# Tying first products behind dense groups, and putting the next stage's groups in front of the states

## The chip, the core and the metric

The kernel runs on one core of a Trainium2 chip. TensorE (PE) multiplies, VectorE (DVE), ScalarE (ACT) and GpSimd (POOL) work on elements, and SyncE's queue (SP) issues the DMAs. The metric is the device time of one execution in microseconds (us); smaller is better.

## The reference

A trunk of two layers works on a sequence of 1040 rows (16 learned meta rows, then 1024 of x) of 1024 float32 numbers. Each layer does

- `h = h + W_out [HGRN2 heads | gated DeltaNet heads | S5 groups](RMSNorm(h) W_in)`
- `h = h + W2 relu(RMSNorm(h) W1)^2`, with a hidden width of 4096

and a last RMSNorm follows. `W_in` has 3336 columns: four blocks of 256 for HGRN2 (query, forget, input, gate), four of 512 for the DeltaNet (q, k, v, gate z), 8 columns for its rates a and b, and 256 for S5. q, k and v go through a causal convolution of four taps and a silu. The DeltaNet solves, for each chunk, a triangular system made of its keys and decays, and then passes a 128x128 state from chunk to chunk. HGRN2 passes a 64x64 state for each head, S5 a diagonal complex one.

## The kernel before, in words

Activations lie with features on partitions and time along the row. The sequence is cut into two blocks of T=520 columns (b=0, 1), and each layer l is run for one block after the other, so that there are four stages, written (l,b). A block has NW=5 windows of W=104 columns.

**Dense groups.** A product with float32 inputs is made of three fp32r products: each operand is split into a rounded part and a rest (`split`), and `columns` (line 490) adds `wh*xh + wh*xl + wl*xh` over eight 128-row pieces into one of two PSUM buffers `pd`: 48 matmuls to a group. Weights come in granules of 128x512 (`granule`), a DMA, a cast on ACT and a subtraction on DVE or POOL for each. Each stage has 26 groups from `W_in`: 2 for S5 (`in_s5`), 12 for the convolutions (`in_conv`), 4 gates z and 2 HGRN2 gates (`in_gate`), 6 for HGRN2 (`in_hgrn`); `in_rows` makes a and b. `out_mlp` adds `W_out` (8 groups) and the MLP.

**What goes by way of DRAM.** The convolved q, k and v (`qkvd`), the gates (`gated`), the rate rows (`rowd`), the DeltaNet's matrices (`MAd`, and `XD` with the solved diagonal blocks), the HGRN2 rows (`hd`), S5's rows (`ud`, `yd`) and the mixers' outputs (`ydr`) are stored to DRAM and loaded again in other layouts.

**The mixers.** `gdn_begin` (line 816) loads the rate rows and transposes them on PE (line 832); it fills `gtok`, `gsc`, `diag` and `MAd`, which exist once. `gdn_decay` makes the matrices of a window and a pair of heads (10 items), `gdn_solve` (line 912) solves 26-wide diagonal blocks on DVE and stores them to `XD`. `gdn_state` (line 951) does the rest for each of the 10 items: it loads, transposes k and v (lines 973 and 974), multiplies the matrix by the solved blocks (line 987), copies a transposed quarter on ACT (line 993), and carries the state of its pair from window to window; its result is stored at line 1054. `hgrn` (line 1179) begins with three products with a constant block matrix (line 1205). `s5_layer` (line 336) makes a layer's S5 matrices, mostly on DVE; `s5` runs beside the state items.

**The order.** The program's calls give priorities, and a planner makes each engine's queue from them: of the instructions whose inputs are ready by its own clock and for whose tile a buffer is free, the first in program order goes next. Each engine then runs its queue in that order, and waits where data come later than planned. Tiles of one tag share a number of buffers: `s` 6, `mt` 11, `qt` 2, `D2` 3, `ys` 3, `xh` and `xl` 8 each. `after` (line 127) can tie one instruction of an engine behind another in the queue, without a wait.

**The stages.** `block` runs (0,0), (0,1) and (1,1): `normed_rows` makes a stage's normed and split operands (16 tiles), `projection` runs its groups and mixers, and `states` its DeltaNet and S5 states. Then `out_mlp(0,0)` follows; `projection(1,0)` is interleaved with `out_mlp(0,1)`; then `states(1,0)`, stage (1,1), and `out_mlp(1,b)` for both blocks. The operands of a stage lie in `xh` and `xl`, but those of (1,0) in the idle tiles of the states (`spare_operands`: `mt`, `qt` and `D2`). A function `early`, traced inside `projection(0,0)`, loads x of block 1 through tiles `s`, turns it on PE (line 1306) and saves it.

## Time and profile before

| | |
|---|---|
| median of 3 runs | 2977.9 us (2974.53 to 2978.24) |
| the profiled execution | 2977.42 us |
| its span, first to last instruction | 2975.6 us |
| PE busy in the span | 2809.2 us (94%) |
| DVE, ACT, POOL busy | 58%, 44%, 27% |
| mean granted clock of PE | 0.97 |

The page gives busy times over the whole span, and then 40 slices with a digit for tenths. PE is busy nearly everywhere, but not in the first slices, around the ninth, and where the DeltaNet's solve of a stage stands. A granted clock of 0.5 is 1.2 GHz, of 1.0 is 2.4 GHz; a value between is a mean over a stretch.

### The profile page before, as it was taken

To read this page: it belongs to the slowest core of one execution; us is meant where nothing else is said; L and a number is where in the kernel's file an instruction comes from. 1 tells how busy PE (TensorE), PEld (TensorE's weight loads), DVE (VectorE), ACT (ScalarE), POOL (GpSimd) and SP (SyncE) were. 2 spreads that over 40 slices of the span, in tenths; PEclk is the share of its full clock that TensorE was granted. 3 is DMA by queue.
4 is the path that set the end of the run, shared out by engine and by line. 5 is a ranking of instruction groups with operands and counts; after the bars stand their busy time and mean duration, and the time that the engine had idled before them with its cause. 6 is when DMAs were issued, how large, how long until landed. Compare 5 with 4: busy or idle time off the path is not lost.

```text
span 2975.6 us, 60318 instructions
## 1 busy us (share of the span) xinstructions
PE 2809.2 (94%) x23513; PEld 2623.8 (88%) x23513; DVE 1715.3 (58%) x3505; ACT 1308.8 (44%) x2690; POOL 816.0 (27%) x793
## 2 busy tenths in 40 slices
PE   7797899979999999998999998999899999999998
PEld 6697798878999999998999988997777788999998
DVE  7788885775532246668765677669645323622224
ACT  5455475534443344443443446554344333533332
POOL 0000532154634420000020320112636444144441
PEclk8898999989999999999999999999899999999999
DMA  5666655744433344444543456564534333533332
GB/s 152 187 150 180 168 147 153 192 88 127 121 88 108 91 139 122 127 125 103 160 125 101 120 161 161 156 195 116 133 112 113 89 105 96 162 93 93 92 91 82
DMA packets 641610, 381.17 MB, mean 128 GB/s; under 512 B 166239, under 2 KB 599237, under 8 KB 641325
## 3 DMA queue, kind: packets, MB, share of 16 engines
q1 hardware_dynamic: 641325, 377.31, 46.0%
q8 instruction: 186, 3.05, 0.4%
q14 instruction: 99, 0.81, 0.1%
HBM read 308.52 MB, written 70.43 MB: 127 GB/s over the span
## 4 chain that ended last, share of the span: by engine, by line
PE 76%; DVE 12%; DMA 6%; issue 2%; ACT 2%; POOL 1%; SPq 1%; DVEq 0%; ACTq 0%; POOLq 0%
PE pd L125 65%; PE mxt L125 7%; DVE mh L113 4%; PE mxh L125 3%; DVE s L116 1%; DVE wl L113 1%; DVE s L113 1%; DMA nt<-rowd 1%; DMA ys<-ydr 1%; DMA XD<-diag 1%; ACT s L110 1%; DMA nh<-rowd 1%; DMA wr<-in_mlp_w_dram 0%; DVE h L113 0%; DVE mt L113 0%
## 5 line engine op out<-in xcount | busy, mean ns | idle before, releaser
L460 ACT CAST wh<-wr 128x512 fp32r<-128x512 f32 x776 | 479.8, 619 | 963.2 <-PE pd L125 883.2
L125 PE MATMUL pd<-xh,wh 128*128 128x260 f32 (+4 forms) x3336 | 751.6, 298 | 26.9 <-ACT wh L460 7.2
L125 PE MATMUL pd<-xl,wh 128*128 128x260 f32 (+4 forms) x3336 | 751.6, 298 | 4.5 <-DVE xl L113 2.6
L125 PE MATMUL pd<-xh,wl 128*128 128x260 f32 (+2 forms) x3288 | 737.4, 297 | 1.8 <-DVE wl L113 1.0
L113 POOL TENSOR_TENSOR wl<-wr,wh 128x512 fp32r<-128x512 f32 x368 | 488.7, 1329 | 730.4 <-ACT wh L460 697.4
L125 PEld LDWEIGHTS pd<-xh,wh 128*128 128x128 f32 (+1 forms) x3336 | 531.4, 190 | 47.3 <-ACT wh L460 11.5
L125 PEld LDWEIGHTS pd<-xl,wh 128*128 128x128 f32 (+1 forms) x3336 | 533.0, 190 | 20.4 <-DVE xl L113 3.4
L125 PEld LDWEIGHTS pd<-xh,wl 128*128 128x128 f32 x3288 | 526.1, 191 | 17.0 <-POOL wl L113 2.2
L125 PE MATMUL pd<-uh,wh 128*128 128x260 f32 (+1 forms) x1928 | 456.8, 305 | 17.3 <-DVE h L113 16.3
L125 PE MATMUL pd<-uh,wl 128*128 128x260 f32 (+1 forms) x1928 | 455.8, 304 | 0.0
L125 PE MATMUL pd<-ul,wh 128*128 128x260 f32 (+1 forms) x1928 | 453.8, 304 | 1.0 <-DVE ul L113 1.0
L113 DVE TENSOR_TENSOR h<-h,pd 128x520 f32<-128x520 f32 (+2 forms) x296 | 200.0, 677 | 327.7 <-PE pd L125 325.5
L113 DVE TENSOR_TENSOR wl<-wr,wh 128x512 fp32r<-128x512 f32 x408 | 285.2, 700 | 105.1 <-ACT wh L460 91.1
L125 PEld LDWEIGHTS pd<-uh,wh 128*128 128x128 f32 x1928 | 310.9, 190 | 33.5 <-DVE h L113 10.4
L125 PEld LDWEIGHTS pd<-uh,wl 128*128 128x128 f32 x1928 | 310.9, 190 | 14.2
L125 PEld LDWEIGHTS pd<-ul,wh 128*128 128x128 f32 x1928 | 310.6, 190 | 14.1 <-DVE ul L113 1.6
L110 ACT ACTIVATE s<-s 128x520 f32<-128x520 f32 (+3 forms) x431 | 272.2, 636 | 111.5 <-DVE s L121 51.8
L116 DVE SCALAR_TENSOR_TENSOR s<-pd,r 128x520 f32<-128x520 f32 (+2 forms) x121 | 83.5, 691 | 249.6 <-PE pd L125 249.0
L113 DVE TENSOR_TENSOR s<-s 128x520 f32<-128x520 f32 (+3 forms) x199 | 137.9, 696 | 51.0 <-ACT s L110 48.3
L113 DVE TENSOR_TENSOR ul<-s,uh 128x520 fp32r<-128x520 f32 (+1 forms) x129 | 94.7, 737 | 115.3 <-ACT uh L460 114.8
L113 POOL TENSOR_TENSOR nt<-nt 128x208 f32<-128x208 f32 x80 | 58.0, 725 | 348.7 <-ACT nt L110 209.6
L403 POOL MEMSET mh<- 128x512 f32 x2 | 1.1, 526 | 499.0 <-DVE RT L113 299.0
(275 smaller groups left out, 3527.0 us busy)
## 6 DMA issues: line engine op xcount, KB each, us to landing
wr<-in_mlp_w_dram SPq DMA_DIRECT2D x512, 256.0 KB
wr<-in_w_in_dram SPq DMA_DIRECT2D x208, 256.0 KB
wr<-in_w_out_dram SPq DMA_DIRECT2D x64, 256.0 KB
qkvd<-s SPq DMA_DIRECT2D x48, 260.0 KB
win<-qkvd SPq DMA_DIRECT2D x40, 312.0 KB
hdr<-h SPq DMA_DIRECT2D x32, 260.0 KB
mh<-qkvd SPq DMA_DIRECT2D x40, 208.0 KB
hd<-s SPq DMA_DIRECT2D x32, 260.0 KB
```

Of the source, the lines that this page charges most:

```text
L110: return self.nc.scalar.activation(out, in_, func, **kw)
L113: return (eng or self.nc.vector).tensor_tensor(out, a, b, op)
L116: return self.nc.vector.scalar_tensor_tensor(out, a, s, b, op0, op1)
L125: return self.nc.tensor.matmul(out, lhsT, rhs, start=start, stop=stop, **kw)
L403: nc.gpsimd.memset(z, 0.0)
L460: self.nc.scalar.copy(hi, src)
```

## The change

1. `columns` keeps its last matmul in `self.dense`, and a new `pin` ties an instruction behind it in PE's queue. Tied are: the transposes of the rate rows in `gdn_begin`; in `gdn_state` the transposes of k and the first product of the first item alone; and the three block products at the start of `hgrn`.
2. In `projection`, `gdn_begin` comes behind the first two convolutions instead of ahead of them; a gate z follows every two of the first eight convolutions; `s5_layer` stands behind the last four; both `in_hgrn` stand ahead of the HGRN2 gates and mixers.
3. The first groups of the next stage are traced in front of the states: `in_s5` of (0,1) before `states(0,0)`, two `W_out` groups of `out_mlp(0,0)` before `states(0,1)`, `in_s5` of (1,1) before `states(1,0)`, two `W_out` groups of `out_mlp(1,0)` before `states(1,1)`. `block` is gone; its parts stand in `run`.
4. Stage (0,0) puts its operands in the spare tiles, and its sum of squares is made on PE: 16 products with the matrix of ones into PSUM, in place of seven additions on DVE and two such products.
5. x of block 1 is loaded through tiles `ys` instead of `s`.

```diff
@@ -128,6 +128,11 @@
         self.tc.add_manual_dep(later.ins, first.ins.name,
                                mybir.DependencyInfo(mybir.DependencyClass.NoSync, mybir.DependencyReason.DATA),
                                reason="accumulation groups of one bank")
+
+    def pin(self, ins):
+
+        self.after(ins, self.dense)
+        return ins
 
     def tl(self, pool, shape, tag, bufs, dt=F32):
         return pool.tile(shape, dt, tag=tag, name=tag, bufs=bufs)
@@ -494,8 +499,8 @@
             wh, wl = wts[k // 4]
             for i, (w, x) in enumerate(((wh, xh), (wh, xl), (wl, xh))):
                 for c, cs in runs.items():
-                    self.mm(ps[:, c, :cs.stop - cs.start], w[:, k % 4, :], x[k][:, cs],
-                            start=(k == 0 and i == 0), stop=(k == kn - 1 and i == 2))
+                    self.dense = self.mm(ps[:, c, :cs.stop - cs.start], w[:, k % 4, :], x[k][:, cs],
+                                         start=(k == 0 and i == 0), stop=(k == kn - 1 and i == 2))
         return ps
 
     def operand(self, tag):
@@ -507,16 +512,28 @@
             for _ in range(bufs):
                 yield self.tl(self.sp, [128, T + HIST], tag, bufs, F32R)
 
-    def normed_rows(self, h, wcol, b, spare=None, acc=None):
+    def normed_rows(self, h, wcol, b, spare=None, acc=None, first=False):
 
         nc = self.nc
         xs = [], []
-        if acc is None:
-            acc = self.s()
+        self.squares, self.r = acc, None
+        if first:
+            self.squares = []
+            for k in range(KD):
+                self.squares.append(self.s())
+                self.act(self.squares[k], h[k], AF.Square)
+                if k == 0:
+                    ps = self.tl(self.pd, [128, 2, 512], "pd", 2)
+                for c in range(2):
+                    self.mm(ps[:, c, :HN], self.K["ones"], self.squares[k][:, self.run_of(c)], start=(k == 0), stop=(k == KD - 1))
+            self.r = self.tl(self.sp, [128, T], "r", 1)
+            self.act(self.half(self.r), ps[:, :, :HN], AF.Ln, scale=1.0 / D, bias=EPS)
+            self.act(self.r, self.r, AF.Exp, scale=-0.5)
+        elif acc is None:
+            self.squares = acc = self.s()
             for k in range(KD):
                 self.square(acc, h[k], k)
-        self.squares, self.r = acc, None
-        r = self.scale("t" if spare else None)
+        r = self.scale("t" if spare and not first else None)
         if b == 0:
             self.hist = self.tl(self.big, [128, KD, HIST], "hist", 1)
         for k in range(KD):
@@ -725,14 +742,6 @@
                     return
             yield
 
-    def block(self, l, b, h, hook=None, first=False, acc=None):
-
-        xs = self.normed_rows(h, 8 * l, b, acc=acc)
-        if first:
-            self.save_h(b, h)
-        trace(self.projection(l, b, xs, hook, first))
-        self.states(l, b)
-
     def projection(self, l, b, xs, hook=None, first=False):
 
 
@@ -746,40 +755,46 @@
         g["rows"] = self.in_rows(l, b, xs)
         yield MIX
         g["qkv"] = self.QKV = self.tl(self.dr, [12, 128, T], "qkvd", 2)
-        self.gdn_begin(l, b, g)
         for p in range(2):
-            for i in (2 * p, 2 * p + 1, 4 + 2 * p, 5 + 2 * p):
+            for n, i in enumerate((2 * p, 2 * p + 1, 4 + 2 * p, 5 + 2 * p)):
                 self.in_conv(l, b, xs, i)
                 yield DENSE
+                if p == 0 and n == 1:
+                    self.gdn_begin(l, b, g)
+                if n % 2:
+                    z = 2 * p + n // 2
+                    self.in_gate(l, xs, C_GZ + 128 * z, g["z"][z])
+                    yield DENSE
             for _ in pipeline([self.gdn_decay(g, w, p) for w in range(NW)], GAP_DECAY):
                 yield MIX
         self.gdn_solve()
         self.gdn_scales()
-        if b == 0:
-            self.s5_layer(l)
         if hook:
             trace(hook)
         for i in range(8, 12):
             self.in_conv(l, b, xs, i)
             yield DENSE
-        for i in range(4):
-            self.in_gate(l, xs, C_GZ + 128 * i, g["z"][i])
-            yield DENSE
+        if b == 0:
+            self.s5_layer(l)
+        hd = []
+        for j in range(2):
+            hd.append(self.in_hgrn(l, xs, j))
+            yield 3 * DENSE
+        self.Y = self.YS[b]
         for j in range(2):
             if j and (l, b) != (1, 0):
                 self.grp = "t"
                 self.loaded = self.s5_load(0, us[0])
                 self.grp = "h"
-            hd = self.in_hgrn(l, xs, j)
-            yield 3 * DENSE
             self.in_gate(l, xs, C_HG + 128 * j, g["z"][4 + j])
             yield DENSE
-            for _ in self.hgrn(l, b, j, hd, g["z"][4 + j]):
+            for _ in self.hgrn(l, b, j, hd[j], g["z"][4 + j]):
                 yield MIX
         self.mixed = g, us
 
     def states(self, l, b):
         g, us = self.mixed
+        self.Y = self.YS[b]
         self.grp = "t"
         trace(pipeline([self.gdn_state(l, g, w, p) for w in range(NW) for p in range(2)], GAP_STATE),
               self.lead(self.s5(l, b, us), AHEAD_S5))
@@ -829,7 +844,7 @@
         for w0, n in ((0, 4), (4, 1)):
             ps = self.mps()
             for i in range(n):
-                nc.tensor.transpose(ps[:W, i * 68:(i + 1) * 68], rows[:68, (w0 + i) * W:(w0 + i + 1) * W], self.ident[:68, :68])
+                self.pin(nc.tensor.transpose(ps[:W, i * 68:(i + 1) * 68], rows[:68, (w0 + i) * W:(w0 + i + 1) * W], self.ident[:68, :68]))
             for i, c in enumerate((0, 36, 64)):
                 nc.scalar.copy(tok[:, w0:w0 + n, i], ps[:W, :n * 68].rearrange("p (a b) -> p a b", a=n)[:, :, c:c + 4])
         sc = self.tl(self.sp, [W, NW, 4, 4], "gsc", 1)
@@ -970,14 +985,18 @@
         ps = self.mps()
         ps4 = ps[:W].rearrange("p (a b c) -> p a b c", a=2, b=2)
         for h in range(2):
-            nc.tensor.transpose(ps4[:, 0, h, :], qkv[:, 2 + h, :], self.ident)
+            first = nc.tensor.transpose(ps4[:, 0, h, :], qkv[:, 2 + h, :], self.ident)
+            if w + pair == 0:
+                self.pin(first)
             nc.tensor.transpose(ps4[:, 1, h, :], qkv[:, 4 + h, :], self.ident)
         kv = self.m()[:W, :512].rearrange("p (a b c) -> p a b c", a=2, b=2)
         self.tt(kv, ps4, sc[:, w, 0:2, hs].unsqueeze(3).to_broadcast([W, 2, 2, 128]), ALU.mult)
         yield
         ps = self.mps()
         for h in range(2):
-            self.mm(p2(ps)[:, h, :], M[:, h, :], XT[:, h, :])
+            first = self.mm(p2(ps)[:, h, :], M[:, h, :], XT[:, h, :])
+            if w + pair == 0:
+                self.pin(first)
         Pm = self.n([W, 2, W])
         self.tt(Pm, p2(ps), K["lev"].unsqueeze(1).to_broadcast([W, 2, W]), ALU.mult)
         yield
@@ -1202,7 +1221,7 @@
         for src, dst, val in ((P[:, :HN], ho[:, :HN], v[:, :HN]), (P[:, HN:], ho[:, HN:], v[:, HN:]), (f, g_, odd(v, 0))):
             ps = self.mps()
             for i, part in enumerate(self.parts(src)):
-                self.mm(ps[:, :HN], K["blk"], part, start=(i == 0), stop=(i == 1))
+                self.pin(self.mm(ps[:, :HN], K["blk"], part, start=(i == 0), stop=(i == 1)))
             self.tt(dst, ps[:, :HN], val, ALU.mult)
             yield
         self.tt(odd(ho, 1), odd(ho, 1), g_, ALU.add, eng=nc.gpsimd)
@@ -1294,7 +1313,7 @@
         for w in range(NW):
             t0 = b * T + w * W - NMETA
             for k0 in (0, 4):
-                xt = self.s()[:W, :512]
+                xt = (self.tl(self.sp, [128, T], "ys", 3) if b else self.s())[:W, :512]
                 cs = slice(128 * k0, 128 * k0 + 512)
                 if t0 < 0:
                     nc.sync.dma_start(xt[0:NMETA, :], self.ins["meta"][:, cs])
@@ -1503,15 +1522,25 @@
         trace(self.load_x(0, h))
         self.ready = {(0, col): self.in_weights(0, col) for col in (C_SU, C_SU + 128)}
         self.setup_norms()
-        self.block(0, 0, h, early(), True)
-        self.block(0, 1, nxt[1])
-        h = self.get_h(0)
+        xs = self.normed_rows(h, 0, 0, self.spare_operands(), first=True)
+        self.save_h(0, h)
+        trace(self.projection(0, 0, xs, early(), True))
+        xs = self.normed_rows(nxt[1], 0, 1)
+        nxt = self.projection(0, 1, xs)
+        next(nxt)
+        self.states(0, 0)
+        trace(nxt)
         ys = []
 
         def before():
             self.low = None
             ys.append(self.y_operands(1, 0))
-        trace(self.out_mlp(0, 0, h, before=before))
+        h = self.get_h(0)
+        nxt = self.out_mlp(0, 0, h, before=before)
+        for _ in range(2):
+            next(nxt)
+        self.states(0, 1)
+        trace(nxt)
         self.low = None
         xs = self.normed_rows(h, 8, 0, self.spare_operands(), self.acc)
         self.save_h(0, h)
@@ -1528,14 +1557,24 @@
         trace(rest)
         acc = self.acc
         self.save_h(1, h)
+        xs = self.normed_rows(h, 8, 1, acc=acc)
+        nxt = self.projection(1, 1, xs)
+        next(nxt)
         self.states(1, 0)
-        self.block(1, 1, h, acc=acc)
+        trace(nxt)
+
         for b in range(NB):
-
             self.take(512 if b == 0 else T)
             h = self.get_h(b)
             self.steps = None
-            trace(self.out_mlp(1, b, h, b == 1))
+            nxt = self.out_mlp(1, b, h, b == 1)
+            if b == 0:
+                for _ in range(2):
+                    next(nxt)
+                self.take(T)
+                self.states(1, 1)
+                self.take(512)
+            trace(nxt)
             self.low = None
             self.finish(b, h, self.steps)
```

## Rows read from the trace of the kernel before

**Rows 1.** The page's span, busy times, and slices of PE, POOL and PE's clock.

```profile
span 2975.6 us, 60318 instructions
...
PE 2809.2 (94%) x23513; PEld 2623.8 (88%) x23513; DVE 1715.3 (58%) x3505; ACT 1308.8 (44%) x2690; POOL 816.0 (27%) x793
...
PE   7797899979999999998999998999899999999998
...
POOL 0000532154634420000020320112636444144441
PEclk8898999989999999999999999999899999999999
```

**Rows 2.** Who PE waited for, whole span: us in total, times, longest.

```profile
PE pd L1306 <- DMA s<-in_x_dram: 15.0, 6, 8.9
PE mxt L125 <- DMA mt<-MAd: 13.1, 2, 8.5
PE mxh L832 <- DMA mh<-rowd: 11.1, 4, 8.0
```

**Rows 3.** Timeline, 20 to 31 us, sum of squares: start, us, engine, line, tiles.

```profile
25.93 0.70 DVE L113 TENSOR_TENSOR s<-s 128x520 f32<-128x520 f32 x1
...
26.69 2.10 PE L125 MATMUL pd<-s,ones 128*128 128x260 f32 x4 [6.20 <-DVE s L113]
...
29.52 0.58 ACT L110 ACTIVATE r<-pd 128x520 f32<-128x520 f32 x1
```

**Rows 4.** Timeline of PE at 1833 us: the same products elsewhere.

```profile
1833.42 1.04 PE L125 MATMUL mxt<-mt,ones 128*128 128x260 f32 x4
```

**Rows 5.** Windows of 10 us: PE, PEld, DVE, ACT, POOL busy, PEclk, DMA.

```profile
110.00:120.00 10.00, 3.07 (x16) 2.61 (x16) 10.00 (x28) 5.64 (x17) 0.00 (x0) 0.58 0.56 153
120.00:130.00 10.00, 5.19 (x24) 3.85 (x24) 4.56 (x15) 3.88 (x13) 0.00 (x0) 0.50 0.81 229
130.00:140.00 10.00, 7.14 (x41) 6.52 (x40) 4.63 (x16) 2.92 (x14) 0.00 (x0) 0.55 0.72 156
```

**Rows 6.** Timeline of SP, 117 to 132 us: loads of x.

```profile
118.96 0.82 SPq L1303 DMA_DIRECT2D s<-in_x_dram  x2
```

**Rows 7.** Windows of 10 us at the end of (0,0)'s groups.

```profile
250.00:260.00 10.00, 1.41 (x5) 0.72 (x5) 9.77 (x18) 6.50 (x16) 0.00 (x0) 0.58 0.10 28
260.00:270.00 10.00, 5.34 (x17) 3.79 (x18) 7.26 (x12) 5.87 (x13) 0.00 (x0) 0.50 0.54 176
```

**Rows 8.** Timeline of SP: last store of `s5_layer`; last store of `states(0,0)`.

```profile
305.14 0.54 SPq L456 DMA_DIRECT2D D<-D  x1
...
553.35 0.37 SPq L1054 DMA_DIRECT2D ydr<-nt  x1
```

**Rows 9.** Window of 10 us at the rate rows of (1,1).

```profile
1820.00:1830.00 10.00, 2.03 (x13) 1.81 (x12) 4.88 (x10) 2.58 (x9) 0.00 (x0) 0.76 0.48 125
```

**Rows 10.** Timeline of PE: first product (line 987) of `states(1,0)`.

```profile
1732.83 0.53 PE L125 MATMUL mxt<-mt 104*104 104x104 f32 x4
```

**Rows 11.** Timeline of ACT: line 993, once an item, in `states(1,0)`.

```profile
1755.20 0.23 ACT L993 COPY nt<-mxt 52x104 f32<-52x104 f32 x1
1782.77 0.24 ACT L993 COPY nt<-mxt 52x104 f32<-52x104 f32 x1
1841.30 0.24 ACT L993 COPY nt<-mxt 52x104 f32<-52x104 f32 x1 [1.30 <-PE mxt L991]
...
1971.39 0.24 ACT L993 COPY nt<-mxt 52x104 f32<-52x104 f32 x1
```

**Rows 12.** Timeline of SP: second `in_s5` of (1,1); last store of `states(1,0)`.

```profile
1791.22 0.35 SPq L161 DMA_DIRECT2D ud<-s  x1
...
1994.42 0.55 SPq L1054 DMA_DIRECT2D ydr<-nt  x1
```

**Rows 13.** Timeline of DVE: five like products of the solves of (0,1) and (1,0).

```profile
630.13 7.61 DVE L113 TENSOR_TENSOR mh<-nh,Tm 80x507 f32<-80x507 f32 x5
...
1386.36 4.43 DVE L113 TENSOR_TENSOR mh<-nh,Tm 80x507 f32<-80x507 f32 x5
```

## The prediction, made before the changed kernel ran

> **What bounds the kernel now.** I read the busy times and slices first. PE works 2809.2 of 2975.6 us [rows 1], so all that can be won without removing products is 166.4 us of idle PE, and the time its products lose at the half clock; in the slices both lie mostly at the start, in the first eighth. Next I read whom PE waited for. Three DMAs stand out, each waited for in the middle of PE's queue by a product that the planner placed too early: x of block 1 (15.0 us), `MAd` (13.1) and the rate rows (11.1) [rows 2]. Then I went through the trace in windows, to see in each hole what else was at its limit, since a hole in which DVE is full does not close when PE's wait goes. Last I looked for the chains that let the next big supply of dense groups begin: stage (0,0) leads by way of `s5_layer`, whose last store is at 305.14, to `states(0,0)`, which store last at 553.35 [rows 8]; `states(1,0)` store last at 1994.42 [rows 12]. Only then can the `W_out` groups of either layer's block 0 have all their operands. A hole closed before such a point is won only if the chain comes sooner too.
>
> **1. Sum of squares on PE.** Before, seven additions of 0.70 us stand on DVE, the last ends at 26.63, the products with ones take 2.10 us at the half clock, and the normalizer starts at 29.52 [rows 3]. After, 16 products run instead of 2: eight times the work. At full clock the same pair takes 1.04 us [rows 4], so all sixteen take between 8.3 and 16.8 us. They can start with the first square, which was there before the additions began at 26.6 − 4.9 = 21.7, say at 21. Result: between 29 and 38 in place of 28.8. Against that, PE works without a break before the first dense group, so that group should no longer begin at the half clock, and DVE loses 4.9 us of work. Bounds −5 to +8; I take **−2**, near the full-clock end.
>
> **2. x of block 1 through `ys`.** From 110 to 140 PE is busy 3.07 + 5.19 + 7.14 = 15.4 us of 30, at a granted clock near 0.54 [rows 5]. The loads go out from 118.96 on [rows 6], when tiles `s` come free from the convolutions, and PE's queue is blocked behind their transposes. The ten loads themselves stay, in SP's one queue; with three buffers of their own they can be issued whenever SP passes them, though a load that waits for its `ys` buffer holds the weight granules behind it. All the idle is 14.6 us, and the products at half clock cost about 7 more: lower end −21. But DVE was busy 10.00 + 4.56 + 4.63 of these 30 us, and in the first ten it was the full engine, so only its 10.8 idle us can be won. Upper end +3, if three buffers in place of six make the loads trickle. I take **−11**.
>
> **3. Spare operands for (0,0).** Operands of (0,1) no longer wait for the last groups of (0,0). Between 250 and 270 PE is busy 6.75 us of 20; DVE 17.03 [rows 7]. PE could win 13.2, DVE leaves 3.0. I take **−3**, bounds −13 and 0. The spare tiles are those of the states, but these start only behind `s5_layer` anyway, and the last readers of the spare operands, the HGRN2 gates, are dense groups without a wait of their own.
>
> **4. Rate rows tied behind two convolutions.** In (1,1) PE is busy 2.03 us of 10 in the window from 1820, mostly because of the longest wait for rate rows, 8.0 us [rows 2, 9]. Two groups in front cover it; what queues behind the transposes (the decays) needs them anyway. About 1.5 us go back through the clock (0.76 there). In (0,1) `gtok` comes free only with the last state, far behind the convolutions, so there the tie does nothing. I take **−9**; bounds −13 (all 11.1 and the clock) and 0.
>
> **5. Ties in `gdn_state` and `hgrn` at the other stages.** The product that waits 8.5 us for `MAd` [rows 2] belongs to (0,1), and the other one, 4.6 us of the 13.1, to (1,1). Their tie is to the second `W_out` group. In (0,1) the operands of that group are there soon after 553.35 [rows 8], while the solve that feeds the waiting product still runs at 630 [rows 13]. The group is out of the queue long before, and a tie behind something done moves nothing. **0**; lower end −13, the case in which the planner saves these groups up.
>
> **6. `states(1,0)` behind `in_s5` of (1,1).** Here the tie acts. The first item's product ran at 1732.83 [rows 10], as filler beside the end of the MLP; now it stands behind a group whose output was stored at 1791.22 [rows 12]: up to 58 us later. These items are a chain: from the third of the ten to the last, (1971.39 − 1841.30)/7 = 18.6 us an item [rows 11]. But from the first to the third it was 1755.20 to 1841.30, 86 us, where two times 18.6 = 37 us would do: the normalization, S5's own end and the rate-row stall lay between. Starting 58 us late and needing up to 49 less, the chain ends 9 to 58 us late; and only pair 0 is tied, so pair 1's items can go ahead, which takes the delay towards nothing. Bounds 0 and +58. Whatever it is comes through in full, since behind 1994.42 the next groups wait for this chain. I take **+7**, near the 9, since the steady 18.6 us hold for eight of the ten items, and a little less for pair 1.
>
> **7. Order inside the stages.** Gates z between convolutions, both `in_hgrn` first, `s5_layer` later: the same instructions and DMAs, in an order in which a light drain (gate) follows two heavy ones on DVE. `s5_layer` moves past convolutions that ran ahead of most of it anyway. **0**, bounds −8 and +12. The upper end is from the solves: five like DVE products took 7.61 us in (0,1), in a slice where POOL is half busy, and 4.43 in (1,0), where POOL is idle [rows 1, 13], 1.7 times as much; if all 17 DVE us of the two windows of [rows 7] came to stand beside POOL, that would be 12 us. The Trainium skill (SBUF — State Buffer, Who interferes with whom) has the rule: a DVE instruction with two SBUF inputs contends with a GpSimd instruction that reads SBUF. By that rule a later `s5_layer`, beside the POOL work of `hgrn(0,0)`, is a loss of those 12 us; the order of calls, `s5_layer` ahead of `hgrn`, speaks against it.
>
> **Sum.** −2 −11 −3 −9 +0 +7 +0 = −18. The profiled execution took 2977.4 us, of which 1.8 lie outside the span; it is 0.5 below the median, so 2977.9 − 18 = **2960**.
>
> **Rivals.** *A: the ties do all they say.* The planner leaves two groups in front of each first product, also in (0,1) and (1,1): the 13.1 us for `MAd` go, and the late start of step 6 costs nothing, 2960 − 13 − 7 = 2940, with the rest of step 2 some 2933. For it: the waits are real and in-queue [rows 2]. Against: step 5. *B: slower.* `states(1,0)` start 58 us late and pair 1 does not go ahead, because the waiting items hold the buffers; little of the 49 us is caught up. Step 6 then costs about 45 instead of 7: 2998. It turns to slower when step 6 exceeds the 25 us of the other steps. For it: the chain's end meets the end of the dense supply. Against: the first items were slow because of their company. *C: nothing arrives.* Steps 1 to 3 win 16 us of PE time early, but `s5_layer` ends no sooner than 305, `states(0,0)` no sooner than 553, and PE waits there instead: 2960 + 16 = 2976. For it: DVE is full at 110 and at 250 [rows 5, 7]. Against: its idle 10.8 us.
>
> **How the numbers follow.** This measurement can tell about 0.2% (6 us) from no change. Forecast 0.46, its own range 2940 to 2975, of which 0.05 lies within 6 us of before; A 0.19; B 0.18; C 0.17, of which 0.03 faster, 0.10 the same, 0.04 slower. Faster 0.41 + 0.19 + 0.03 = 0.63; same 0.05 + 0.10 = 0.15; slower 0.18 + 0.04 = 0.22. The range for all reaches from inside A to inside B, 2924 to 2995.
>
> **What would show it.** Step 1: a normalizer start near 29 and a first dense group at full clock. Step 2: no wait for `in_x` over 2 us, and block 1's transposes spread over the groups. Step 3: the normalization of (0,1) inside the groups of (0,0), and no hole behind their end. Step 4: the wait for rate rows below 3 us in all. Step 5: waits for `MAd` as before in (0,1) and (1,1). Step 6: the first product at line 987 of `states(1,0)` behind that stage's `in_s5`, and the last store not over 10 us later, counted from the end of the MLP. The prediction is wrong if PE idles more than 15 us ahead of `W_out` of either block 0 (B or C), or if the holes near the solves close too (A).

## The result, and the profile after

The changed kernel takes 3004.2 us (median of 6 runs, 3000.8 to 3010.5) against 2979.8 us of the kernel before in the same runs: a ratio of 1.0082, interval [1.0071, 1.0094]. It is slower by 24 us, where 18 us less was forecast and 2995 was the top of the range. The page of the changed kernel begins so (compare [rows 1]):

```profile
span 3004.1 us, 60347 instructions
...
PE 2836.9 (94%) x23541; PEld 2648.2 (88%) x23541; DVE 1708.5 (57%) x3498; ACT 1309.7 (44%) x2690; POOL 805.5 (27%) x793
...
PE   8897999889999999999799999999899999999998
...
PEclk8998999889999999999999999998999999999999
```

PE's busy time grew by 27.7 us with 28 more records, and its idle time is 167.2 us where it was 166.4. Two things are mixed in this. The 28 records are the new products of step 1, which ran in a stretch where PE had idled before (in [rows 3] they are 4 records and 2.10 us):

```profile
18.65 10.27 PE L125 MATMUL pd<-s,ones 128*128 128x260 f32 x32 [0.33 <-DVE h L1328]
32.07 1.24 PE L125 MATMUL pd<-mt,wh 128*128 128x264 f32 x4 [3.16 <-ACT mt L550]
```

In the first 40 us PE is busy for 28.73 us instead of 21.97. Behind them it idles 7.5 us longer than before and is busy 20.9 us longer, with two records fewer. So most of the loss shows as busy time, where it is easily missed: products that run at the half clock are busy for twice as long (2.10 against 1.04 us in [rows 3, 4]). So I cut both executions at the same four events (`states(0,1)` done, out_mlp(0,1) done, `states(1,0)` done, `states(1,1)` done) and at the first output store. Before (columns as in [rows 5]):

```profile
894.00:1756.00 862.00, 838.82 (x7504) 824.66 (x7502) 496.86 (x968) 356.70 (x661) 135.25 (x136) 0.99 0.43 121
1756.00:1994.00 238.00, 224.65 (x1814) 214.61 (x1815) 164.73 (x323) 136.06 (x300) 32.59 (x39) 0.98 0.63 168
1994.00:2386.00 392.00, 373.41 (x2578) 297.35 (x2578) 227.01 (x448) 166.77 (x375) 177.34 (x173) 0.97 0.44 118
2386.00:2548.00 162.00, 161.68 (x769) 132.42 (x768) 58.36 (x91) 61.59 (x104) 67.80 (x54) 1.00 0.39 118
```

After:

```profile
902.00:1761.00 859.00, 829.34 (x7391) 816.89 (x7391) 488.27 (x942) 354.07 (x656) 130.73 (x129) 0.99 0.43 120
1761.00:2026.00 265.00, 253.49 (x1983) 238.51 (x1983) 176.78 (x356) 142.24 (x313) 38.51 (x46) 0.94 0.60 163
2026.00:2401.00 375.00, 353.68 (x2463) 281.02 (x2463) 213.48 (x432) 159.60 (x357) 170.16 (x169) 0.95 0.43 116
2401.00:2576.00 175.00, 174.68 (x830) 142.82 (x829) 62.52 (x99) 66.90 (x114) 72.84 (x58) 1.00 0.38 116
```

Up to the end of out_mlp(0,1) the changed kernel has lost 5 us. From there to the first output store it takes 265 + 375 + 175 = 815 us where 238 + 392 + 162 = 792 did: 23 us more. Two things are in it. The stretch up to the end of out_mlp(0,1) ran 113 products fewer (7504 to 7391) and became only 3 us shorter; they run later instead, at 838.8/7504 = 0.11 us each some 12 us. And the granted clock fell in both stretches up to `states(1,1)`: one minus the clock, times the length, is 238 x 0.02 + 392 x 0.03 = 17 us before and 265 x 0.06 + 375 x 0.05 = 35 us after. That is 18 us at most, as the column is rounded and a part of it lies over idle PE.

The place is seen in windows of 10 us about the end of `states(1,0)`. The changed kernel:

```profile
2000.00:2010.00 10.00, 8.19 (x58) 6.52 (x56) 4.86 (x12) 4.93 (x12) 0.62 (x1) 1.00 0.60 141
2010.00:2020.00 10.00, 8.31 (x32) 6.91 (x33) 3.32 (x10) 3.05 (x9) 1.87 (x3) 0.56 0.31 82
2020.00:2030.00 10.00, 4.59 (x32) 3.94 (x30) 5.20 (x16) 4.23 (x13) 0.62 (x1) 0.84 0.63 163
2030.00:2040.00 10.00, 7.85 (x26) 6.14 (x27) 8.00 (x23) 4.29 (x13) 0.00 (x0) 0.50 0.71 196
```

The kernel before, 10 us earlier in its run:

```profile
1990.00:2000.00 10.00, 10.00 (x88) 9.76 (x87) 9.54 (x28) 6.06 (x18) 0.64 (x1) 1.00 0.68 201
2000.00:2010.00 10.00, 9.45 (x46) 7.34 (x44) 8.97 (x22) 6.19 (x16) 0.00 (x0) 1.00 1.02 310
2010.00:2020.00 10.00, 8.55 (x40) 7.23 (x41) 8.54 (x18) 6.24 (x14) 0.00 (x0) 0.83 0.71 180
```

Before, the chain of `states(1,0)` ends at 1994 while PE still has groups of (1,1), and the `W_out` groups take over. After, the groups of (1,1) and the first few `W_out` products are used up at about 2004, the chain ends at 2026, and in between PE has mostly the small products of the items: it is partly idle, its clock falls to 0.56 and, after 2030, to 0.50, and `W_out` products run at that clock. The timeline of SP and PE in the changed kernel gives the chain (compare [rows 8, 10, 12]): the last store of `s5_layer` and of `states(0,0)`; the last store of `h` by out_mlp(0,1); the first product of `states(1,0)`; the second `in_s5` of (1,1); the last store of `states(1,0)`.

```profile
318.65 0.55 SPq L461 DMA_DIRECT2D D<-D  x1
...
563.45 0.36 SPq L1073 DMA_DIRECT2D ydr<-nt  x1
...
1760.78 0.34 SPq L166 DMA_DIRECT2D hdr<-h  x1
...
1787.15 0.53 PE L125 MATMUL mxt<-mt 104*104 104x104 f32 x4
1787.79 0.46 SPq L166 DMA_DIRECT2D ud<-s  x1
...
2025.77 0.36 SPq L1073 DMA_DIRECT2D ydr<-nt  x1
```

The other holes of the changed kernel, first by whom PE waited for, as in [rows 2]:

```profile
PE mxt L125 <- DMA mt<-MAd: 13.1, 2, 9.0
...
PE pd L125 <- DVE s L113: 9.5, 1, 9.5
...
PE mxh L847 <- DMA mh<-rowd: 5.5, 3, 2.6
...
PE pd L1325 <- DMA s<-in_x_dram: 2.3, 2, 2.0
...
PE pd L1325 <- DMA ys<-in_x_dram: 1.4, 1, 1.4
```

Then by windows, as in [rows 5, 7, 9]:

```profile
110.00:120.00 10.00, 10.00 (x87) 10.00 (x87) 10.00 (x25) 6.62 (x19) 0.00 (x0) 1.00 0.63 161
...
130.00:140.00 10.00, 7.13 (x60) 6.56 (x58) 8.16 (x17) 7.61 (x18) 0.00 (x0) 1.00 0.66 173
140.00:150.00 10.00, 3.96 (x20) 3.37 (x21) 3.19 (x11) 1.84 (x9) 0.00 (x0) 0.54 0.74 210
150.00:160.00 10.00, 7.69 (x48) 6.77 (x48) 8.49 (x30) 4.98 (x22) 0.00 (x0) 0.67 0.68 195
...
240.00:250.00 10.00, 2.64 (x23) 2.43 (x21) 9.80 (x43) 8.05 (x16) 0.00 (x0) 0.83 0.59 145
250.00:260.00 10.00, 3.31 (x8) 2.11 (x8) 9.90 (x27) 5.29 (x13) 0.52 (x1) 0.50 0.48 111
260.00:270.00 10.00, 9.58 (x68) 9.58 (x69) 9.91 (x29) 2.87 (x7) 0.53 (x1) 0.82 0.48 145
...
1820.00:1830.00 10.00, 7.13 (x51) 6.59 (x51) 6.79 (x11) 4.70 (x14) 3.77 (x5) 0.85 0.66 187
```

The window from 240 in the kernel before, which stands ahead of those of [rows 7]:

```profile
240.00:250.00 10.00, 7.51 (x63) 7.30 (x61) 9.88 (x35) 4.42 (x8) 0.00 (x0) 1.00 0.72 174
```

The waits that the change was aimed at did fall: for x from 15.0 to 3.7 us, for rate rows from 11.1 to 5.5. The holes did not go with them. The one from 110 to 140 stands at 130 to 160 now, the one from 250 to 270 at 240 to 260.

### The profile page after: what moved, and what is told of

It reads as the page before. It is cut to its first block, busy times and chain, and to the rows that moved or that the text cites. A ratio compares the mean times of both kernels' runs of the same rounds, so it can differ in the third digit from the quotient of the medians.

```text
span 3004.1 us, 60347 instructions
## 1 busy us (share of the span) xinstructions
PE 2836.9 (94%) x23541; PEld 2648.2 (88%) x23541; DVE 1708.5 (57%) x3498; ACT 1309.7 (44%) x2690; POOL 805.5 (27%) x793
## 4 chain that ended last, share of the span: by engine, by line
PE 77%; DVE 11%; DMA 6%; issue 3%; ACT 2%; SPq 0%; POOL 0%; DVEq 0%; ACTq 0%; POOLq 0%
PE pd L125 65%; PE mxt L125 8%; DVE mh L113 3%; PE mxh L125 3%; DVE s L116 1%; DVE wl L113 1%; DVE s L113 1%; ACT s L110 1%; DMA XD<-diag 1%; DMA nh<-rowd 1%; DVE h L113 0%; DMA mh<-rowd 0%; DVE mt L113 0%; DMA rowd<-s 0%; DMA nt<-rowd 0%
## 5 line engine op out<-in xcount | busy, mean ns | idle before, releaser
L125 PE MATMUL pd<-xh,wh 128*128 128x260 f32 (+3 forms) x2904 | 665.2, 301 | 12.6 <-DVE s L116 4.6
L125 PE MATMUL pd<-xl,wh 128*128 128x260 f32 (+3 forms) x2904 | 662.8, 300 | 6.2 <-DVE xl L113 3.5
L125 PE MATMUL pd<-xh,wl 128*128 128x260 f32 (+2 forms) x2872 | 656.0, 300 | 1.0 <-POOL wl L113 1.0
L125 PEld LDWEIGHTS pd<-xh,wh 128*128 128x128 f32 (+1 forms) x2904 | 466.6, 191 | 31.3 <-ACT xh L550 4.9
L125 PEld LDWEIGHTS pd<-xl,wh 128*128 128x128 f32 (+1 forms) x2904 | 468.3, 191 | 22.1 <-DVE xl L113 4.3
L125 PEld LDWEIGHTS pd<-xh,wl 128*128 128x128 f32 x2872 | 463.5, 192 | 16.6 <-POOL wl L113 2.1
L125 PE MATMUL pd<-mt,wh 128*128 128x264 f32 (+3 forms) x1188 | 206.9, 295 | 24.9 <-DVE h L113 5.6
L125 PEld LDWEIGHTS pd<-mt,wh 128*128 128x128 f32 (+1 forms) x1188 | 173.6, 195 | 28.3 <-issue 9.1
```

What stands on the lines that cost most here:

```text
L125: return self.nc.tensor.matmul(out, lhsT, rhs, start=start, stop=stop, **kw)
```

## The experiments

Each ratio is against runs of the kernel before on the same chip. The edits are cut to the lines that matter: `...` marks a gap, and lines that only serve others (`pin`, `self.dense`, `self.Y`) are left out. Landmarks are from one profiled execution each. M is the last store of `h` by out_mlp(0,1). It fell between 1754.6 and 1769.3, and between 1756.2 and 1763.5 even in kernels whose program text differs only behind it, so times near the end are counted from M. The table collects all kernels, by where `states(1,0)` stand in the program and how soon their first product ran.

| kernel | first product, from M | last store of `states(1,0)`, from M | ratio |
|---|---|---|---|
| before | -23 | 238 | 1 |
| b1, b2 (before + one part) | -23, -23 | 238, 239 | 1.0012, 0.9998 |
| h2 (before, items put ahead) | -26 | 231 | 0.9993 |
| f1, g4: behind `in_s5`, no state tie | -24, -24 | 241, 240 | 1.0012, 1.0008 |
| b3: states first, new inner order | -1 | 239 | 1.0001 |
| e1, e6: states first, all ties | -1, -1 | 241, 242 | 1.0032, 1.0019 |
| o1: states first, all ties, old inner order | 0 | 253 | 1.0061 |
| g3: behind `in_s5`, new inner order, no tie | -1 | 258 | 1.0069 |
| e2, g2: behind `in_s5`, no state tie | -1, -1 | 251, 253 | 1.0051, 1.0075 |
| f2: behind `in_s5` and tied | 24 | 260 | 1.0072 |
| the changed kernel | 26 | 265 | 1.0082 |
| e3, e4, e5, g1 (changed - one part) | 26, 25, 26, 27 | 262, 260, 267, 263 | 1.0094, 1.0079, 1.0088, 1.0095 |
| h1 (changed, items put ahead) | 26 | 268 | 1.0102 |

From the last store of `states(1,0)` to the end of the span it is 971 to 981 us in all twenty kernels, so what a kernel loses here it has lost by that store. From M to the end of the span it is 1210 to 1219 us in the nine kernels whose chain ends by 242, and 1223 to 1243 in the eleven whose chain ends at 251 or later.

**Where `states(1,0)` stand: e1 and f1.** e1 is the changed kernel with the states in front again.

```diff
+        self.states(1, 0)
         xs = self.normed_rows(h, 8, 1, acc=acc)
         nxt = self.projection(1, 1, xs)
-        next(nxt)
-        self.states(1, 0)
         trace(nxt)
```

> The changed kernel with one place undone: states(1,0) are traced ahead of the normalization and of in_s5 of (1,1), as before; all ties stay. Theory 'late chain' (the 28 us are lost because the states of (1,0) begin behind in_s5 of (1,1), so that W_out of layer 1's block 0 gets its operands late): the last store of states(1,0) comes 20 to 32 us sooner, and the time falls from 3004 to 2972 to 2984. Rival 'clock' (the loss is spread: PE at the half clock more often, no one place): the time stays within 8 us of 3004.

Measured: 1.0032 [1.0017, 1.0046]. The timelines of PE and SP give the first product and the last store of `states(1,0)` in e1:

```profile
1754.00 0.53 PE L125 MATMUL mxt<-mt 104*104 104x104 f32 x4
...
1996.11 0.46 SPq L1073 DMA_DIRECT2D ydr<-nt  x1
```

Its windows behind that end:

```profile
2000.00:2010.00 10.00, 8.38 (x63) 7.75 (x62) 8.70 (x22) 6.71 (x18) 0.00 (x0) 1.00 0.85 227
2010.00:2020.00 10.00, 10.00 (x57) 8.36 (x57) 9.97 (x25) 6.92 (x17) 0.00 (x0) 1.00 0.92 273
```

The hole at the end of the chain is gone, and with it more than half of the loss (0.82% to 0.32%). f1 is the opposite: the kernel before with that one move.

```diff
-        self.states(1, 0)
-        self.block(1, 1, h, acc=acc)
+        xs = self.normed_rows(h, 8, 1, acc=acc)
+        nxt = self.projection(1, 1, xs)
+        next(nxt)
+        self.states(1, 0)
+        trace(nxt)
+        self.states(1, 1)
```

> The kernel before, with one edit: normalization and in_s5 of (1,1) are traced in front of states(1,0); no tie anywhere. Theory 'two parts' (the place of states(1,0) behind in_s5 costs by itself, and the tie adds to it): the last store of states(1,0) comes 10 to 18 us later than 1994, at 2004 to 2012, and the ratio is 1.003 to 1.006. Rival 'the tie is needed' (the planner takes the first items as filler anyway, as soon as a buffer is free): last store at 1994 to 1999, ratio 0.999 to 1.002.

Measured: 1.0012 [0.9997, 1.0027], no difference that can be measured. The first item still ran as filler beside the MLP, at 1739.47. So the move is needed for most of the loss, but does not make it by itself.

**Move and tie: f2.** f1 and the state ties of the changed kernel, nothing else.

```diff
-            nc.tensor.transpose(ps4[:, 0, h, :], qkv[:, 2 + h, :], self.ident)
+            first = nc.tensor.transpose(ps4[:, 0, h, :], qkv[:, 2 + h, :], self.ident)
+            if w + pair == 0:
+                self.pin(first)
...
-            self.mm(p2(ps)[:, h, :], M[:, h, :], XT[:, h, :])
+            first = self.mm(p2(ps)[:, h, :], M[:, h, :], XT[:, h, :])
+            if w + pair == 0:
+                self.pin(first)
```

> As f1, and the first item of gdn_state is tied behind the last dense group as in the changed kernel (in the other stages that group is long done). Theory 'two parts': 12 to 16 us more than f1, last store of states(1,0) at 2016 to 2026, ratio 1.007 to 1.011: this alone is then the whole loss of the changed kernel. Rival 'the rest of the change has its share' (stage (0,0) is 8 us late in the changed kernel and passes that on): last store at 2008 to 2014, ratio 1.003 to 1.006.

Measured: 1.0072 [1.0053, 1.0091]: these two edits alone give nearly the whole loss. The first product and the last store in f2:

```profile
1782.61 0.53 PE L125 MATMUL mxt<-mt 104*104 104x104 f32 x4
...
2017.98 0.36 SPq L1065 DMA_DIRECT2D ydr<-nt  x1
```

**Without the state ties: e2.** The changed kernel less the two `pin` of `gdn_state`.

```diff
-            if w + pair == 0:
-                self.pin(first)
```

> The changed kernel without the ties in gdn_state (the first item's transposes and first product are free); the order of the calls stays. Theory 'order' (a place behind in_s5 in program order is what makes states(1,0) late): within 5 us of 3004. Rival 'tie' (the tie of the first item makes them late, as my step 6 has it): the first product of states(1,0) runs near 1735 again, their last store near 1996, and the time falls to about 2980.

Measured: 1.0051 [1.0031, 1.0072]; the chain ends 251 us behind M. That is neither the 265 of the changed kernel nor f1's 241, so the tie delays the chain, and something else does too. The next four look for that.

**The other ties: g1 and g2.** g1 leaves out the ties in `hgrn` alone, g2 those and the state ties.

```diff
-                self.pin(self.mm(ps[:, :HN], K["blk"], part, start=(i == 0), stop=(i == 1)))
+                self.mm(ps[:, :HN], K["blk"], part, start=(i == 0), stop=(i == 1))
```

> The changed kernel without the ties of the three block products in hgrn; the ties of the states and of the rate rows and every order stay. Measure: from the last store of h by out_mlp(0,1) to the last store of states(1,0), 238 us before, 265 in the changed kernel, 260 with order and state tie alone. Theory 'order and state tie' (they are the loss, the HGRN2 ties add nothing): 258 to 266, ratio 1.006 to 1.009. Rival 'HGRN2 ties' (they pushed 110 products behind the MLP, and these fill PE until the groups run out): 245 to 255, ratio 1.002 to 1.005.

> The changed kernel without the ties of the states and without those in hgrn; the tie of the rate rows and every order stay. With the state ties alone gone the measure was 251 us (238 before, 241 with the order alone) and the ratio 1.0051. Theory 'HGRN2 ties have the rest': 238 to 244, ratio 1.000 to 1.003. Rival 'the new order inside (1,1), or its late rate rows, has the rest': 248 to 254, ratio 1.003 to 1.006.

Measured: 1.0095 [1.0074, 1.0116] and 1.0075 [1.0049, 1.0102]. Neither is better than the same kernel with these ties (1.0082 and 1.0051). The ties in `hgrn` have no part in it that shows; the rest lies in the orders or the late rate rows.

**The inner order alone, and with the move: b3 and g3.** b3 is the kernel before with the new order inside the stages (`gdn_begin` stays ahead); g3 is f1 with the same.

```diff
             for n, i in enumerate((2 * p, 2 * p + 1, 4 + 2 * p, 5 + 2 * p)):
                 self.in_conv(l, b, xs, i)
                 yield DENSE
+                if n % 2:
+                    z = 2 * p + n // 2
+                    self.in_gate(l, xs, C_GZ + 128 * z, g["z"][z])
+                    yield DENSE
...
+        if b == 0:
+            self.s5_layer(l)
+        hd = []
+        for j in range(2):
+            hd.append(self.in_hgrn(l, xs, j))
+            yield 3 * DENSE
```

> The kernel before with the new order inside the stages alone (gates z between the convolutions, s5_layer behind the last convolutions, both in_hgrn first); gdn_begin, the ties, x, the operands and the sum of squares as before. Theory 'order' (this order is why stage (0,0) ran 8 us late in the changed kernel): last store of s5_layer at 313 to 320 instead of 305, of states(0,0) at 560 to 566 instead of 553, ratio 1.001 to 1.004. Rival 'another part of the change': 303 to 308 and 551 to 556, ratio 0.998 to 1.001.

> The kernel before with in_s5 of (1,1) in front of states(1,0) and the new order inside the stages; no tie, gdn_begin ahead of the convolutions as before. Each of the two alone gave 1.0012 and 1.0001. Theory 'the two orders together': measure 247 to 254, ratio 1.003 to 1.006, with a hole in PE ahead of the last store of states(1,0). Rival 'orders cost nothing without a tie': 238 to 244, ratio 0.999 to 1.002.

Measured: b3 1.0001 [0.9983, 1.0019], g3 1.0069 [1.0045, 1.0093]. In both the first product runs only at the end of the MLP, 23 us later than before. With the states first in the program the chain still ends at 239; behind `in_s5` it ends at 258, and the hole is there without any tie. The first product and the last store in g3:

```profile
1760.34 0.53 PE L125 MATMUL mxt<-mt 104*104 104x104 f32 x4
...
2018.63 0.52 SPq L1059 DMA_DIRECT2D ydr<-nt  x1
```

The windows about that end in g3:

```profile
2010.00:2020.00 10.00, 7.16 (x48) 5.56 (x46) 5.38 (x12) 5.45 (x15) 1.25 (x2) 1.00 0.68 174
2020.00:2030.00 10.00, 5.38 (x20) 4.12 (x21) 9.12 (x27) 4.24 (x13) 0.00 (x0) 0.61 0.86 230
```

So there are two ways to a late first item, and in these kernels the chain's end suffers only where the items also stand behind `in_s5` (o1, below, is the exception). The first products of the ten items show where a late start is caught up. From the first to the third it is 62.1 us before and 43.8 in b3, but 58.5 in g3, which is b3 with the move; 48.6 to 49.9 with the states in front (e1, e6), but 54.7 and 57.8 behind `in_s5` and tied (f2 and the changed kernel). From the third to the fourth it is 49 to 59 us in all seven, however late the third is. b3 also had `s5_layer` end at 318 and `states(0,0)` at 561, without a loss in total: the late stage (0,0) costs nothing in the end.

**Rate rows: b1 and g4.** `gdn_begin` behind two convolutions with its transposes tied, in the kernel before (b1) and in f1 (g4).

```diff
+                if p == 0 and n == 1:
+                    self.gdn_begin(l, b, g)
...
-                nc.tensor.transpose(ps[:W, i * 68:(i + 1) * 68], rows[:68, (w0 + i) * W:(w0 + i + 1) * W], self.ident[:68, :68])
+                self.pin(nc.tensor.transpose(ps[:W, i * 68:(i + 1) * 68], rows[:68, (w0 + i) * W:(w0 + i + 1) * W], self.ident[:68, :68]))
```

> The kernel before with one part of the change alone: gdn_begin behind two convolutions, its transposes tied. My step 4 says 9 us faster (2966 to 2970), with waits for rate rows under 3 us. Rival 'chain': the 8 us wait at (1,1) goes, but the states of (1,0) still store last at 1994, and the time stays within 4 us of before.

> The kernel before with in_s5 of (1,1) in front of states(1,0), and gdn_begin behind two convolutions with its transposes tied behind the last group; nothing else. Theory 'the late rate rows' (with the tie's group now truly in front, the wait at the rate rows falls from 11 us to under 4, the groups are used up sooner, and the chain does not end sooner): measure 240 to 248, ratio 1.001 to 1.004, with more PE idle ahead of the last store of states(1,0) than in the kernel before. Rival 'the wait is won': ratio 0.996 to 0.999.

Measured: 1.0012 [0.9999, 1.0024] and 1.0008 [0.9995, 1.0022]. PE's waits for rate rows in b1:

```profile
PE mxh L838 <- DMA mh<-rowd: 9.0, 3, 7.6
```

The same in g4:

```profile
PE mxh L840 <- DMA mh<-rowd: 9.0, 2, 7.5
```

The longest wait, 8.0 us before, did not go in either, so neither shows what winning it would be worth.

**x through `ys`: b2**, that one line in the kernel before.

```diff
-                xt = self.s()[:W, :512]
+                xt = (self.tl(self.sp, [128, T], "ys", 3) if b else self.s())[:W, :512]
```

> The kernel before with one part alone: x of block 1 through ys instead of s. My step 2 says 11 us faster (2964 to 2968), the hole from 110 to 140 mostly closed. Rival 'hole moves' (the transposes wait for a turn among the dense groups, not for their data, and the hole comes where DVE next lags): within 4 us of before, and a hole of 10 us or more in PE between 110 and 170.

Measured: 0.9998 [0.9985, 1.0010]. The products that turn x ran 13 to 7 us sooner (the first at 110.45 instead of 123.28, the last at 131.50 instead of 138.49), but from 110 to 140 PE was busy for 17.2 us instead of 15.4, no more. Over the whole span it waited for DVE's `s` 21.7 us, 12.6 at the longest, where it had waited 9.5.

**Parts of the changed kernel put back: e3, e4, e5, e6, o1.** e3 sets `s5_layer` ahead of the last convolutions, e4 gives (0,0) the operands and squares of before, e5 sets the gates z behind the last convolutions, e6 sets `states(0,0)` and `states(1,0)` in front (as e1, for both layers). The edit of e4:

```diff
-        xs = self.normed_rows(h, 0, 0, self.spare_operands(), first=True)
+        xs = self.normed_rows(h, 0, 0)
```

> The changed kernel with s5_layer back ahead of the last four convolutions, in both layers; all else stays. Theory 's5_layer' (stage (0,0) became 8 to 14 us later because its S5 set-up moved behind convolutions 8 to 11): its last store returns from 319 to about 305, states(0,0) end at 550 instead of 563, and 8 to 12 us of the time go, to about 2994. Rival 'solve' (the states were late because gates z stand ahead of the decays and the solve): the last store of s5_layer stays at 315 or later and the time within 4 us of 3004.

> The changed kernel with the operands and the sum of squares of (0,0) as before (xh and xl, additions on DVE). Theory 'spare pays' (my step 3 and 1: 3 + 2 us): slower than the changed kernel by 3 to 15 us, since in_s5 of (0,1) waits for operands again. Rival 'spare costs nothing and wins nothing' (DVE is full there): within 4 us of 3004.

> The changed kernel with the four gates z back behind the last convolutions; all else stays. Theory 'solve': the decays and the solve of (0,0) come 10 us sooner again (blocks of XD stored at 206 instead of 216), and the time falls by about 8 us, to 2996. Rival 's5_layer': the time stays within 4 us of 3004.

> The changed kernel with states(0,0) and states(1,0) traced ahead of the next stage's normalization and in_s5; the other two places and all ties stay. Theory 'both chains' (what is left of the loss after states(1,0) are put first comes from states(0,0), which end at 563 instead of 553 for the same reason): the last store of states(0,0) returns to 553 and the time falls to 2970 to 2976, as before. Rival 'set-up' (states(0,0) are late because s5_layer ends at 319 instead of 305): the store stays at 560 or later and the time at 2980 to 2986.

Measured: 1.0094 [1.0067, 1.0121], 1.0079 [1.0063, 1.0096], 1.0088 [1.0064, 1.0112], 1.0019 [1.0003, 1.0035]. In e3 `s5_layer` still ended at 320. In e4 nothing was lost with the spare operands. In e5 the solve of (0,0) was stored from 207 on (before: 206), in place of 216, and the total did not move. In e6 `states(0,0)` stored last at 567, so their place is not what makes them late. o1 is e6 with the inner order of before.

> The changed kernel with states(0,0) and states(1,0) in front again and the order inside the stages as in the kernel before; the sum of squares on PE, x through ys, the spare operands, the late gdn_begin and the ties stay. Theory 'order': the leftover 0.2% goes, last store of states(0,0) at 550 to 557, ratio 0.996 to 1.001; were the first steps of the prediction worth their 16 us, the ratio would be 0.993 to 0.996. Rival 'another part of the change': states(0,0) at 560 to 567 still, ratio 1.001 to 1.004.

Measured: 1.0061 [1.0041, 1.0080], and 253 us from M, where e6 had 242. This fits neither theory, nor the pattern of the table, since its states stand first. Its profile has no hole at the end of the chain; a wait of 8.3 us for rate rows is back. The delay has a place: the third item's first product runs 46 us from M, where e6 had 48, and the fourth 107, where e6 had 98, and the wait stands between them. That the wait makes the delay is not shown, since the kernel before has one of 8.0 us between the same two items. I leave it open.

**Can priority mend it? h1 and h2.** The changed kernel and the kernel before, with the items of `states(1,0)` put ahead in the planner's priority.

```diff
-        trace(pipeline([self.gdn_state(l, g, w, p) for w in range(NW) for p in range(2)], GAP_STATE),
+        items = pipeline([self.gdn_state(l, g, w, p) for w in range(NW) for p in range(2)], GAP_STATE)
+        trace(self.lead(items, 600) if (l, b) == (1, 0) else items,
```

> The changed kernel, with the DeltaNet items of states(1,0) put ahead in the planner's priority (offset 600, as S5 has 200); the ties stay, so the first product cannot run sooner than some 26 us behind the last store of h by out_mlp(0,1). Theory 'chain against supply' (what costs is that the items, being behind in_s5 and its normalization, do not catch up, and the groups of (1,1) run out first): last store 245 to 256 us behind that store of h in place of 265, ratio 1.002 to 1.006. Rival 'the tie itself' (nothing catches up a start that is 50 us late): 262 to 268, ratio 1.007 to 1.010.

> The kernel before, with the DeltaNet items of states(1,0) put ahead in the planner's priority (offset 600). There the first product runs 23 us ahead of that store of h, and PE has groups of (1,1) left when the chain ends at 238. Theory 'chain against supply': an earlier end, 220 to 236, is worth nothing, since no hole stands there: ratio 0.998 to 1.001. Rival 'this chain bounds in the kernel before as well': ratio 0.993 to 0.997.

Measured: h1 1.0102 [1.0070, 1.0134] with the chain's end at 268; h2 0.9993 [0.9976, 1.0010] with 231. The rival was right for h1: priority does not bring back a first product held until 26 us behind M. In h2 the chain ends 7 us sooner and the time does not move. In this one trial an earlier end was worth nothing while groups were left; the later ends of the table cost. No kernel tried beats the kernel before.

## Why the prediction was wrong

**The step that failed is 6**, `states(1,0)` behind `in_s5` of (1,1). It was priced at +7, "near the 9" that a start 58 us late would leave after "needing up to 49 less"; the bounds were 0 and 58. The start stood as written: the tie held the first product until 1787, 54 us later than [rows 10]. The catching up, on which the price rested, came only in part and late. ACT's timeline in the changed kernel shows the like copies of the first three items (compare [rows 11]):

```profile
1799.77 0.24 ACT L1012 COPY nt<-mxt 52x104 f32<-52x104 f32 x1
...
1827.25 0.24 ACT L1012 COPY nt<-mxt 52x104 f32<-52x104 f32 x1
...
1883.88 0.23 ACT L1012 COPY nt<-mxt 52x104 f32<-52x104 f32 x1
```

From the first to the third it is 84.1 us, against 86.1 before and the 37 that I counted on. I had blamed the slow first items on the normalization, S5's end and the rate-row stall; but the stall shrank from 8.0 to 2.6 us and the items stayed as slow, so it was not the stall; which of the others it was, no run tells apart. Counted from M, the first product of the chain runs 49.7 us late, that of the fourth item 38.1, that of the tenth 35.9, and the last store 26.7. The last 9 us were won in the hole, where no groups stood between the products. That "pair 1's items can go ahead" failed too: the second item's result was stored 52 us behind the first's, and 58 behind it before. Rival B had the direction, the place and the catching up that fails; its reason, buffers held by waiting items, was not looked at, and its price, "about 45 instead of 7", was too high. The sign set for it, more than 15 us of idle PE ahead of `W_out`, would not have shown it here: PE idled 11.1 us in the four windows from 2000, and what the fallen clock cost is not in that.

The size: step 6 was to turn the sum when it exceeded 25 us. It measured some 27 us at the end of the chain, 3 of which came back before the end of the span (2025.77 to 3004.1 is 978.3 us, 1994.42 to 2975.6 is 981.2). f2, with its move and tie alone, prices it at 0.72%, 21 us, where +7 was forecast. By itself that would only have cancelled the gains; but these were not there.

**Step 1** (-2): the normalizer started at 28.95 instead of 29.52, as forecast, and the first dense window, 30 to 40, still ran at 0.58 (0.50 before), so the clock part failed: PE did not work "without a break", but idled 3.16 us ahead of the first group, waiting for its operand. e4, which takes the squares and step 3 out, is as slow as the changed kernel. **Step 2** (-11): the waits went, as forecast, but the hole moved behind them to 130 to 160, and b2 gives 0.9998. **Step 3** (-3): 250 to 270 gained 6.1 us of PE time, and 240 to 250 lost 4.9. Rival C's condition held for these three: `states(0,0)` stored last at 563.45, no sooner than 553. At 320 us the changed kernel had run 64 records more, 36 without the 28 of step 1; from there to that store it took 243 us, 18.4 of them idle, where 233 with 8.6 idle had done. What failed in them is one belief, that DVE's idle share in a hole can be won: the products that fill a hole early are missing at the next point where PE waits. That it is the same products is a reading of these counts.

**Step 4** (-9): the window at 1820 rose from 2.03 to 7.13 us of PE, as forecast, and the waits for rate rows fell to 5.5 us, not below 3; nothing came of it. That the groups used there are missing at the end of the chain is my reading; b1 and g4, made to price it, kept the wait. **Step 5** (0) held: 13.1 us of waits for `MAd` before and after, and g1 shows the ties in `hgrn` to be nothing. **Step 7** (0) held alone (b3, 1.0001) and failed beside step 6: g3 against f1 is 1.0069 against 1.0012. I had added terms that act only together: the state tie and the inner order each take away the early start, and the move takes away the precedence that would have made up for it.

What stays open: why the inner order alone holds the first product until M, the 0.6% of o1, and the 0.2 to 0.3% that e1 and e6 keep although their chain ends in time. For the first, the traces show that the last loads of `XD` and `MAd` ahead of it do not come late (1657.94 and 1658.33 in b3, 1655.53 and 1656.81 before), while HGRN2's products of (1,0), which stand ahead of the states in the program, do: their first 64x40 products ran at 1637.91 instead of 1589.59. That these took the places of the first item is not tested.

## What to carry to other kernels

Where a chain of small items must end before the next big supply of dense groups can start, compare two times: when the chain ends, and when the groups that cover it run out. Here being early was worth nothing (h2), and being late cost about one us for each: chain ends from 242 to 268 us behind M go with 1217 to 1243 us from M to the end of the span. A part of that is no idle time, since the clock falls in the hole (0.56 and 0.50 in two windows). An early start as filler and a front place in the order were each enough to end in time in every kernel but o1; an edit that takes one away should be priced with the other also gone, and not as a term by itself.

## What was not expected

PE's total idle time did not show the loss at all: it is equal to within 1 us (166.4 and 167.2), because the new products of step 1 filled 6.8 us of early idle time while 7.5 us came in behind. The clock showed it, 0.94 and 0.95 in the two stretches about the end of the chain in place of 0.98 and 0.97, together with the count of products, 113 fewer in the stage ahead of it.
